# Gates moved into attention, cached values beside the branch products, and a third pass of the second out projection

## The chip, the cores and the metric

The kernel runs on one core of one Trainium2 chip. The metric is the device time in microseconds (us) of the whole program. The core has five engines with queues of their own, each of which works in order: PE multiplies matrices, DVE does element work on vectors, ACT does the same with functions and scales, POOL does it more slowly and also issues transfers, and SP only issues transfers. PE has two clock levels, 1.2 and 2.4 GHz; the profile gives the granted clock of a stretch as a share of the higher one.

## The reference, cut to what matters

One decoder layer, one inference step: a prompt of 1024 tokens and 8 samples of 4 new tokens each, whose earlier 1024 tokens lie in a paged cache.

```
proj   = x @ w_in                      # columns: q k v | HGRN q f i g | gate_a | gate_b
oA     = diff attention, 4 heads       # softmax(q1 k1) - lambda softmax(q2 k2), times v
         # samples: keys and values gathered from cache pages, 8 x 2 pages of each
oB     = HGRN2 recurrence, 4 heads
merged = sigmoid(gate_a) * (oA @ w_branch_a) + sigmoid(gate_b) * (oB @ w_branch_b)
h      = LayerNorm(ALPHA * x + merged @ w_out)
[a|g]  = h @ w_up;  c = causal conv3(a) + b
out    = LayerNorm(ALPHA * h + (gelu(c) * g) @ w_down)
```

Keys, values, the recurrent state and the last rows of the convolution (conv_p, conv_s) are outputs too.

## The kernel before

All data are float32. Each float32 product is made of three products of halves: a tile is split into a high part (`wh`, an ACT cast) and a low part (`wl`, a DVE subtraction), and high x high, low x high and high x low are added up (lines 238 to 240 for projections, 1147 to 1149 and 1248 to 1250 in the feed-forward part).

The kernel is written with a scheduler: the code issues instructions in program order, and the scheduler reorders them on each engine by their place in the program, their readiness as it models them, and the buffers of their pools. What has no buffer waits for one.

The stages follow each other. First come the turning of x, the HGRN heads and the projections, to about 405 us. Then the attention heads 0 to 3, to about 626 us, in which projections of the next head are the only other work for PE. A **gate** is one 128-column piece of gate_a or gate_b for all tokens: `do_gates(1)` issues 72 matmuls and their sigmoid. 16 of them exist. Before, one or two get among the attention heads by the scheduler's own doing and fourteen calls of `do_gates(1)` stand in a loop with the sample attention: in the first seven turns `sample.keys` (eight calls, one for each sample, two page gathers each), in the last seven `sample.values` (again eight). A gather (line 726) is an indirect transfer issued by POOL into the buffers `pg`, of which there are two; a page of values is used by 32 small matmuls (line 803).

The tokens are then worked on in two halves of 512 and 544 columns. `merge(Ot, half)` first makes the branch products (eight steps m, of which each multiplies both branches and adds them under the gates), and then the out projection `merged @ w_out` in two passes over the output columns (`hf` 0 and 1): each pass loads and splits its half of w_out (`w_B`) and goes over the token tiles. A tile's LayerNorm (line 1102, ACT) follows its second pass; the result h is turned, written to DRAM scratch (`hT`) and read again in quadrants for the feed-forward part, which uses seven products of sums of quadrants (B11, T2, B21, B22, T1, T3, T4) instead of eight plain ones. `up` runs over 22 column steps and two token chunks, `down_half` over 22 input steps for each half; its inputs come back from DRAM scratch (`r<-uT`, through two staging tiles). `ln2` is the final LayerNorm. For half 0 it is done by ACT (scale, line 1305) and POOL (gain and offset, lines 1306 and 1307), for half 1 mostly by DVE (lines 1311 and 1312). `conv_out` turns the convolution's last rows, copies them from PSUM to `co` on ACT (two buffers) and writes each `co` with two transfers; it is the last code of the program.

Of the kernel before, what the change touches and what calls it, by code (L numbers as in the profile page):

```python
# [44 lines left out]
def hybrid_step(ctx: ExitStack, tc: tile.TileContext, I, O):  # L45
# [797 lines left out]
    gates = [(3584, m, m) for m in range(8)] + [(4608, m, 8 + m) for m in range(8)]  # L843
# [94 lines left out]
    for i in range(14):  # L938
        do_gates(1)
        for b in range(8 * (i % 7) // 7, 8 * (i % 7 + 1) // 7):  # L940
            (sample.keys if i < 7 else sample.values)(b)
        if i == 6:
            aps.close()
        if i == 11:
            Ot = load_o(*HALVES[0][:2])
    avs.close()
    px.close()
    up[1] = ctx.enter_context(tc.tile_pool(name="upb", bufs=1))
    w2s, ups = ExitStack(), ExitStack()
    wx[0] = w2s.enter_context(tc.tile_pool(name="wx", bufs=1))  # L950

    rp = [ctx.enter_context(rpool("ra")), ups.enter_context(rpool("rb"))]
    h0 = ups.enter_context(rpool("h0"))
# [10 lines left out]
    def operands():  # L964
        c0 = []
        for o in range(7):
            pair = []
            for i in range(2):
                home = {(T4, 0): 0, (T4, 1): 1, (T3, 1): 4}.get((o, i))
                pair.append(h0.tile([128, 4, 256], F32R, name=f"h0_{o}{i}") if home is None else rt(home, (4, 256), F32R))  # L970
# [39 lines left out]
    def merge(Ot, half):  # L1010
# [5 lines left out]
        for m in range(8):  # L1016
            w = wunit([wview(wbb, m * 128, 128), wview(wba, m * 128, 128)])
            ga, gb_ = wide("ae"), wide("c")
            SY.dma_start(gb_[:, :nh], gsc[8 + m][:, th:th + nh])
            SY.dma_start(ga[:, :nh], gsc[m][:, th:th + nh])  # L1020
            for c0, cn in cks:
                cs = slice(c0, c0 + cn)
                pb, pa = pmm(), pmm()
                mm3(pb[:, :cn], [(w[k], (Ot[k][:, 0, cs], Ot[k][:, 1, cs])) for k in range(4)])
                mm3(pa[:, :cn], [(w[k], (Ot[k][:, 0, cs], Ot[k][:, 1, cs])) for k in range(4, 8)])
                V.scalar_tensor_tensor(gb_[:, cs], gb_[:, cs], 1.0, pb[:, :cn], ALU.add, ALU.mult)
                V.scalar_tensor_tensor(ga[:, cs], ga[:, cs], 1.0, pa[:, :cn], ALU.add, ALU.mult)
# [53 lines left out]
        for hf in range(2):  # L1081
            w = w_B(wout, hf * 512, 512)
            late = []
            for t, r in zip(tiles, rr):
                tt, tn = tok(t)
# [11 lines left out]
                if hf == 0:  # L1097
                    continue
# [9 lines left out]
    merge(Ot, 0)  # L1108
    Ot = load_o(*HALVES[1][:2])
    merge(Ot, 1)  # L1110

# [3 lines left out]
    def wcombos(m):  # L1115
# [12 lines left out]
        put(B11, a11)  # L1128
        G.tensor_tensor(s1, a21, a22, ALU.add)
        G.tensor_tensor(s2, s1, a11, ALU.subtract)  # L1130
        put(T2, s2)
        put(B21, a12)
        put(T1, s1)
        G.tensor_tensor(a11, a11, a21, ALU.subtract)
        put(T3, a11)
        G.tensor_tensor(a12, a12, s2, ALU.subtract)
        put(B22, a12)
# [15 lines left out]
    for m in range(NM):  # L1153
# [8 lines left out]
        for c, cn in enumerate(CHUNK):  # L1162
# [18 lines left out]
            V.tensor_tensor(u3, m1, product(w, x, T3, cn), ALU.add)  # L1181
            G.tensor_tensor(gg[:, 1, o:o + cn], u3, m5, ALU.add)
            conv_in(1, u4, product(w, x, B22, cn))
            V.tensor_tensor(gg[:, 0, o:o + cn], u3, product(w, x, T4, cn), ALU.add)
            if m + c == 0:

                while pending:
                    pending.pop(0)()
                for t in (2, 3):
                    tile_operands(t)  # L1190
# [19 lines left out]
    us = ctx.enter_context(rpool("us"))  # L1210
# [5 lines left out]
    def ut(k):  # L1216
# [3 lines left out]
        return qt((0, 1, 2, 3, 4, 5, 8, 9, 10, 11, 6, 7, 12, 13, 14, 15)[k - 6])  # L1220

    def down_half(half):
# [3 lines left out]
        for k in range(NM):  # L1226
            if k % 2 == 0:
                raw = rt(2 + k // 2 % 2, (2, 544))
# [57 lines left out]
        def ln2(i0, i1):  # L1286
# [10 lines left out]
            for i in range(i0, i1):  # L1297
# [4 lines left out]
                np_ = D if i == 4 or not half else 512 if i == 1 else 0  # L1302
# [6 lines left out]
                for c in range(0, D - np_, 512):  # L1309
# [3 lines left out]
                    SY.dma_start(y[:, c], r[:, c])  # L1313

        down((0, 1), cks)
        for m in range(2, KD - 2 if half else KD):
            down((m,), cks)
        if half:
# [6 lines left out]
        else:  # L1325
            ln2(0, 4)

    down_half(0)
    down_half(1)


# [90 lines left out]
```

## Time and profile before

| | |
|---|---|
| device time, median of 3 runs | 1865.85 us (1859.72 to 1867.9) |
| the profiled execution, its own time | 1858.9 us |
| its span in the trace | 1857.1 us |
| PE busy | 1732.4 us, 93% of the span |
| DVE, ACT, POOL busy | 60%, 41%, 32% |
| mean granted PE clock | 0.967 |
| DMA | 213 MB, mean 115 GB/s |

The share of PE is an average over stages with different limits. A busy PE can also be a slow one, so the clock is read beside it; matmuls are pipelined, so their pace is read from how many start in a stretch and not from the duration of one. Idle time of the other engines costs nothing while PE works.

### The profile page before, as it was taken

The page shows a single profiled execution, that of the slowest core. Times are in us where ns is not written, and L with a number is a line of the kernel's source. Part 1 is how long each engine was busy: PE and PEld are TensorE (multiplying, and loading weights), DVE is VectorE, ACT ScalarE, POOL GpSimd, SP SyncE. Part 2 cuts the span into 40 slices and gives each one's busy share as a digit, 9 for nine tenths or more (in the row PEclk, how much of TensorE's full clock was granted, in tenths as well). Part 3 has the DMA queues.
Part 4 walks back from the last instruction along what each step waited for, and adds up shares of the span by engine and source line. Part 5 has one row for each costly group of instructions (what it writes and reads, how often), then busy time and mean ns, then how long its engine had stood idle before and what let it go on. Part 6 is the DMA issues. An engine that isn't in the chain of part 4 may idle for free.

```text
span 1857.1 us, 34326 instructions
## 1 busy us (share of the span) xinstructions
PE 1732.4 (93%) x13412; PEld 1620.2 (87%) x13412; DVE 1117.9 (60%) x2297; ACT 770.1 (41%) x1771; POOL 594.1 (32%) x736
## 2 busy tenths in 40 slices
PE   8999999998998989898979859999999997998995
PEld 8999999997987989786879659999999996887995
DVE  5767555656668555115556777777766776336435
ACT  6466253445646512212243444444434444225222
POOL 0000110432322222112121467766676662003203
PEclk9999999998999999998989969999999998999998
DMA  6120211220210277676566232222322227435543
GB/s 210 35 59 25 81 59 45 85 70 27 78 36 13 98 272 252 235 232 216 162 207 184 64 99 84 84 76 70 92 76 76 70 88 234 127 108 169 157 125 108
DMA packets 214122, 212.99 MB, mean 115 GB/s; under 512 B 11084, under 2 KB 182046, under 8 KB 209864
## 3 DMA queue, kind: packets, MB, share of 16 engines
q1 hardware_dynamic: 189856, 133.95, 23.7%
q0 software_dynamic: 16976, 67.99, 10.5%
q10 hardware_dynamic: 7128, 8.86, 1.4%
q8 instruction: 106, 1.74, 0.4%
q14 instruction: 56, 0.46, 0.1%
HBM read 170.34 MB, written 40.41 MB: 113 GB/s over the span
## 4 chain that ended last, share of the span: by engine, by line
PE 78%; DMA 8%; DVE 4%; issue 4%; ACT 2%; POOL 2%; SPq 0%; ACTq 0%; POOLq 0%; DVEq 0%
PE mm L238 10%; PE mm L239 10%; PE mm L240 10%; PE mm L1147 4%; PE mm L1149 4%; PE mm L1148 4%; PE mm L1250 3%; PE mm L1249 3%; PE mm L1248 3%; PE tp L220 3%; DMA pg<-in_cache_k_dram,idx 2%; PE tp L1147 2%; PE tp L1148 2%; PE tp L1149 2%; PE ps_s L1147 2%
## 5 line engine op out<-in xcount | busy, mean ns | idle before, releaser
L133 DVE TENSOR_TENSOR wl<-raw,wh 128x512 fp32r<-128x512 f32 x370 | 272.4, 743 | 244.1 <-ACT wh L132 229.7
L132 ACT CAST wh<-raw 128x512 fp32r<-128x512 f32 x370 | 222.1, 608 | 295.2 <-PE mm L1249 119.2
L238 PE MATMUL mm<-xh,wh 128*128 128x384 f32 (+1 forms) x560 | 187.2, 335 | 0.3 <-ACT wh L132 0.3
L239 PE MATMUL mm<-xl,wh 128*128 128x384 f32 (+1 forms) x560 | 186.2, 333 | 0.0
L240 PE MATMUL mm<-xh,wl 128*128 128x384 f32 (+1 forms) x560 | 186.1, 333 | 0.0
L238 PE MATMUL mm<-wh,xh 128*128 128x256 f32 x480 | 137.0, 286 | 1.4 <-DVE rb L581 1.3
L239 PE MATMUL mm<-wl,xh 128*128 128x256 f32 x480 | 137.0, 286 | 0.2 <-DVE wl L133 0.2
L240 PE MATMUL mm<-wh,xl 128*128 128x256 f32 x480 | 136.2, 285 | 0.0
L1250 PE MATMUL mm<-q,wl 128*128 128x512 f32 (+2 forms) x384 | 125.7, 329 | 5.2 <-DVE wl L133 5.2
L1248 PE MATMUL mm<-q,wh 128*128 128x512 f32 (+2 forms) x384 | 125.2, 326 | 0.3 <-ACT wh L132 0.3
L1249 PE MATMUL mm<-q,wh 128*128 128x512 f32 (+2 forms) x384 | 125.0, 326 | 0.0
L240 PEld LDWEIGHTS mm<-xh,wl 128*128 128x128 f32 x560 | 105.7, 189 | 3.6 <-issue 3.5
L238 PEld LDWEIGHTS mm<-xh,wh 128*128 128x128 f32 x560 | 105.6, 189 | 2.9 <-issue 2.0
L239 PEld LDWEIGHTS mm<-xl,wh 128*128 128x128 f32 x560 | 105.9, 189 | 2.0 <-issue 1.8
L238 PEld LDWEIGHTS mm<-wh,xh 128*128 128x128 f32 x480 | 91.1, 190 | 2.9 <-issue 1.5
L239 PEld LDWEIGHTS mm<-wl,xh 128*128 128x128 f32 x480 | 91.1, 190 | 1.2 <-DVE wl L133 0.6
L240 PEld LDWEIGHTS mm<-wh,xl 128*128 128x128 f32 x480 | 91.2, 190 | 0.1
L1257 POOL DMA_DIRECT2D c<-hT x24 | 12.9, 539 | 220.4 <-PE tp L220 91.7
L1250 PEld LDWEIGHTS mm<-q,wl 128*128 128x128 f32 x384 | 73.1, 191 | 10.9 <-DVE wl L133 5.6
L1147 PE MATMUL mm<-h,wh 128*128 128x256 f32 x264 | 75.0, 284 | 5.2 <-ACT h L132 5.2
L1248 PEld LDWEIGHTS mm<-q,wh 128*128 128x128 f32 x384 | 73.2, 191 | 5.8 <-ACT wh L132 0.5
L1249 PEld LDWEIGHTS mm<-q,wh 128*128 128x128 f32 x384 | 73.2, 191 | 5.7 <-DVE q L133 0.4
(496 smaller groups left out, 5517.0 us busy)
## 6 DMA issues: line engine op xcount, KB each, us to landing
raw<-in_w_in_dram SPq DMA_DIRECT2D x44, 512.0 KB, 3.8
raw<-in_w_up_dram SPq DMA_DIRECT2D x44, 512.0 KB, 4.9
raw<-in_w_down_dram SPq DMA_DIRECT2D x36, 512.0 KB, 3.9
raw<-in_w_out_dram SPq DMA_DIRECT2D x16, 512.0 KB, 3.5
raw<-in_w_down_dram SPq DMA_DIRECT2D x18, 384.0 KB, 3.5
gsc<-gt ACTq DMA_DIRECT2D x32, 192.0 KB, 2.5
r<-uT SPq DMA_DIRECT2D x22, 272.0 KB, 3.8
uT<-ae POOLq DMA_DIRECT2D x22, 256.0 KB, 2.4
```

Source lines behind the costliest of these rows:

```text
L132: S.copy(h, src)
L133: eng.tensor_tensor(l, src, h.bitcast(F32), ALU.subtract)
L220: PE.transpose(out, in_, ident[:n, :n])
L238: PE.matmul(ps, lhsT=ah, rhs=bh, start=(i == 0), stop=False)
L239: PE.matmul(ps, lhsT=ah, rhs=bl, start=False, stop=False)
L240: PE.matmul(ps, lhsT=al, rhs=bh, start=False, stop=(i == n - 1))
L1147: PE.matmul(ps, lhsT=ah, rhs=bh, start=(k == 0), stop=False)
L1148: PE.matmul(ps, lhsT=ah, rhs=bl, start=False, stop=False)
L1149: PE.matmul(ps, lhsT=al, rhs=bh, start=False, stop=(k == 3))
L1248: PE.matmul(ps, lhsT=ah, rhs=bh, start=(k == 0), stop=False)
L1249: PE.matmul(ps, lhsT=ah, rhs=bl, start=False, stop=False)
L1250: PE.matmul(ps, lhsT=al, rhs=bh, start=False, stop=(k == NM - 1))
```

## The change

Six edits. Three gates are issued after head 0 and two after head 1 of the attention, and the loop of the sample attention has nine gates left: they go with the eight calls for keys and the first two for values. The gates' order changes from all gate_a first to gate_a and gate_b in turn. The other six calls for values are made inside `merge` of half 0, after every second branch step (four) and after two tiles of the out projection's first pass. The out projection of half 1 goes in three passes: columns 0 for tiles 4 and 5, columns 1 for all tiles, columns 0 for tiles 8, 6 and 7; w_out's first half is loaded and split twice for it. The seven products are made in another order. The final LayerNorm of half 0's prompt tiles goes from ACT and POOL to DVE, piece by piece in the turns of half 1's loop, with its stores on POOL's queue. The feed-forward part's staging gets a third tile, and to make room `co` has one buffer instead of two.

```diff
-    gates = [(3584, m, m) for m in range(8)] + [(4608, m, 8 + m) for m in range(8)]
+    gates = [(3584 + 1024 * i, m, 8 * i + m) for m in range(8) for i in range(2)]
...
     attn(0, Q[0], K[0], v[0])
+    do_gates(3)
     K1 = proj_k(1, k_slots())
     vsl = tok_slots()
     attn(1, Q[1], K[1], v[1])
     v = proj_tok(1024, 1, vsl, vs_, O["v_p"], O["v_s"])
+    do_gates(2)
...
-    for i in range(14):
+    steps = [(sample.keys, b) for b in range(8)] + [(sample.values, b) for b in range(8)]
+    def beside(n):
+        for f, b in steps[:n]:
+            f(b)
+        del steps[:n]
+        if len(steps) == 8:
+            aps.close()
+    for n in (2, 1, 1, 1, 1, 1, 1, 1, 1):
         do_gates(1)
-        for b in range(8 * (i % 7) // 7, 8 * (i % 7 + 1) // 7):
-            (sample.keys if i < 7 else sample.values)(b)
...
+        beside(n)
...
-    def merge(Ot, half):
+    def merge(Ot, half, beside=None):
...
+            if beside and m % 2:
+                beside(1)
-        tiles = (8, 4, 5, 6, 7) if half else tiles
+        tiles = (4, 5, 8, 6, 7) if half else tiles
...
-        for hf in range(2):
+        for hf, some in ((0, tiles[:2]), (1, tiles), (0, tiles[2:])) if half else ((0, tiles), (1, tiles)):
             w = w_B(wout, hf * 512, 512)
             for t, r in zip(tiles, rr):
+                if t not in some:
+                    continue
...
-                if hf == 0:
+                if t not in done:
+                    done.add(t)
+                    if beside and t % 2:
+                        beside(1)
                     continue
...
     merge(Ot, 1)
+    tile_operands(2)
...
             S.copy(m1, product(w, x, B11, cn))
-            p6 = product(w, x, T2, cn)
             conv_in(0, m1, product(w, x, B21, cn))
-            V.tensor_tensor(m1, m1, p6, ALU.add)
+            p3 = product(w, x, B22, cn)
             S.copy(m5, product(w, x, T1, cn))
+            V.tensor_tensor(m1, m1, product(w, x, T2, cn), ALU.add)
...
             if k % 2 == 0:
-                raw = rt(2 + k // 2 % 2, (2, 544))
+                j = k // 2 % 3
+                raw = rt(j + 1, (2, 544)) if j else us.tile([128, 2, 544], F32, tag="ur", name="ur")
...
-                co = us.tile([18, 512], F32, tag="co", name="co", bufs=2)[:, :mn * 128]
+                co = us.tile([18, 512], F32, tag="co", name="co")[:, :mn * 128]
...
-                np_ = D if i == 4 or not half else 512 if i == 1 else 0
+                np_ = D if i == 4 else 512 if half and i == 1 else 0
...
-                    SY.dma_start(y[:, c], r[:, c])
+                    (SY if half else G).dma_start(y[:, c], r[:, c])
...
         for m in range(2, KD - 2 if half else KD):
             down((m,), cks)
+            if half:
+                before(m - 2, m - 1)
...
-        else:
-            ln2(0, 4)
-
-    down_half(0)
-    down_half(1)
+        return ln2
+
+    down_half(1, down_half(0))
```

**PE in the last third of attention head 0.** `scp` are the scores, `tp<-s` the turned probabilities (line 220) and their products with the values (line 665), and `mm` projections. Before, from the largest score block on:

```order
2389 L665 MATMUL tp<-s_4123,s_4609 128x128 x4
2390 L637 MATMUL scp<-s_3300,s_3733 128x512
2391 L638 MATMUL scp<-s_3302,qpad_141 128x512
...
2398 L665 MATMUL tp<-s_4123,s_4609 128x128 x2
2399 L220 MATMUL tp<-ident,s_4648 128x128 x7
2400 L637 MATMUL scp<-s_3303,s_3735 128x128
```

And now, at the same block:

```order
2407 L665 MATMUL tp<-s_4123,s_4564 128x128
2408 L220 MATMUL tp<-ident,s_4601 128x128 x4
2409 L239 MATMUL mm<-xl,wh 128x384
2410 L240 MATMUL mm<-xh,wl 128x384
2411 L637 MATMUL scp<-s_3300,s_3733 128x512
...
2415 L238 MATMUL mm<-xh,wh 128x384
2416 L239 MATMUL mm<-xl,wh 128x384
2417 L637 MATMUL scp<-s_3301,s_3734 128x512
```

Between the attention's own matmuls stand gate matmuls (`mm<-xh,wh`) where nothing stood; 216 of them lie in rows 2262 to 2528.

**PE behind the last sample key.** `tp<-pg,aT` are the products with pages of values (32 to a page) and `mm<-q` branch products of half 0. Before, the first two of the values are followed by a gate:

```order
3903 L796 MATMUL tp<-vs__120,an 32x512 x4
3904 L803 MATMUL tp<-pg,aT 32x128 x32
3905 L238 MATMUL mm<-xh,wh 128x384
3906 L239 MATMUL mm<-xl,wh 128x384
```

Now the last gate ends among them, and the branch begins behind two and a half pages:

```order
4240 L796 MATMUL tp<-vs__120,an 32x512 x4
4241 L803 MATMUL tp<-pg,aT 32x128 x32
4242 L239 MATMUL mm<-xl,wh 128x288
...
4252 L240 MATMUL mm<-xh,wl 128x288
4253 L803 MATMUL tp<-pg,aT 32x128 x48
4254 L238 MATMUL mm<-q_8697,wh 128x512
```

The pages moved from between gates of 72 matmuls to a place with 11 matmuls between them, and the later ones into the branch products.

**ACT at the end of the program.** Rows of before, the copies to `co` and the transfers of them:

```order
1496 L216 COPY rt_19534<-tp 128x2x128 x2
1497 L216 COPY co<-tp 18x512 x2
1498 L1283 DMA out_dram<-co 2x512
1499 L1284 DMA out_dram<-co 16x512
1500 L1283 DMA out_dram<-co 2x512
1501 L1284 DMA out_dram<-co 16x512
1502 L216 COPY co<-tp 18x512
```

And now:

```order
1456 L216 COPY rt_19548<-tp 128x2x128 x2
1457 L216 COPY co<-tp 18x512
1458 L1302 DMA out_dram<-co 2x512
1459 L1303 DMA out_dram<-co 16x512
1460 L216 COPY co<-tp 18x512
```

Two copies stood ahead of the first transfer, and now one stands ahead of each pair; the rest of the engine's order at the end is the same.

## Rows read from the trace of the kernel before

**Rows 1.** Stretches: length, busy of each engine (count), PE clock, DMA share, GB/s.

```profile
430.00:460.00 30.00, 22.57 (x135) 19.35 (x134) 19.22 (x76) 15.62 (x50) 7.87 (x17) 0.83 0.07 27
460.00:520.00 60.00, 60.00 (x488) 58.88 (x487) 37.25 (x107) 38.06 (x125) 20.49 (x42) 1.00 0.20 64
520.00:540.00 20.00, 15.86 (x104) 14.05 (x104) 9.51 (x30) 5.24 (x19) 5.61 (x11) 0.83 0.07 27
...
640.00:660.00 20.00, 20.00 (x128) 20.00 (x127) 9.21 (x13) 7.65 (x15) 8.54 (x11) 1.00 0.81 300
...
860.00:890.00 30.00, 30.00 (x132) 24.29 (x130) 21.45 (x30) 9.59 (x17) 9.58 (x7) 1.00 0.67 213
...
1055.00:1110.00 55.00, 25.14 (x156) 23.45 (x155) 43.04 (x62) 23.85 (x50) 38.57 (x35) 0.70 0.31 87
1110.00:1545.00 435.00, 435.00 (x3552) 435.00 (x3552) 321.23 (x576) 193.08 (x427) 288.38 (x312) 1.00 0.26 80
...
1685.00:1720.00 35.00, 28.40 (x202) 27.35 (x201) 25.21 (x32) 16.61 (x27) 19.21 (x9) 0.90 0.47 150
```

**Rows 2.** What PE waited for, whole span: releaser, us in total, times, longest.

```profile
PE tp L1147 <- ACT q L132: 11.7, 1, 11.7
PE tp L803 <- DMA pg<-in_cache_v_dram,idx: 10.1, 3, 7.0
PE mm L1248 <- ACT x L132: 8.4, 1, 8.4
...
PE tp L220 <- DVE s L683: 7.1, 2, 3.6
...
PE mm L1147 <- ACT h L132: 5.2, 1, 5.2
```

**Rows 3.** The same, between 1020 and 1120 us.

```profile
PE tp L220 <- ACT r L1102: 8.0, 1, 8.0
```

**Rows 4.** PE's groups between 757 and 893 us, shapes apart: busy, mean ns.

```profile
L239 PE MATMUL mm<-q,wh 128*128 128x512 f32 x64 | 25.9, 404 | 0.0
L240 PE MATMUL mm<-xh,wl 128*128 128x384 f32 x72 | 24.6, 342 | 0.0
...
L240 PE MATMUL mm<-xh,wl 128*128 128x288 f32 x40 | 11.9, 299 | 0.0
```

**Rows 5.** PE's timeline at one sample's values: start us, duration us, instruction.

```profile
803.19 1.06 PE L796 MATMUL tp<-vs__120,an 32*32 32x512 f32 x8
804.18 1.95 PE L803 MATMUL tp<-pg,aT 128*32 128x128 f32 x64
```

**Rows 6.** Pages of values, 740 to 870 us: landing, then the gather queue's transfers.

```profile
DMA to landing us min/median/max: 5.5/7.5/10.6
...
q0 software_dynamic: 2514, 17.90, 39.5%
```

**Rows 7.** The stretch between 650 and 660 us, columns as in rows 1.

```profile
650.00:660.00 10.00, 10.00 (x65) 10.00 (x64) 5.73 (x8) 3.26 (x7) 2.02 (x5) 1.00 0.92 359
```

**Rows 8.** DMA issues of the page: KB each, median us to landing.

```profile
uT<-ae POOLq DMA_DIRECT2D x22, 256.0 KB, 2.4
```

**Rows 9.** DVE between 1700 and 1720 us, and between 1720 and 1825 us.

```profile
L133 DVE TENSOR_TENSOR wl<-raw,wh 128x512 fp32r<-128x512 f32 x4 | 9.1, 2302 | 0.0
...
L133 DVE TENSOR_TENSOR wl<-raw,wh 128x512 fp32r<-128x512 f32 x38 | 28.4, 746 | 49.9 <-ACT wh L132 48.0 <-PE mm L1249 1.6
```

**Rows 10.** POOL's line 1306 over the span, and DVE's line 1311.

```profile
L1306 POOL TENSOR_TENSOR rt<-rt,lnrow x6: 1270/2460/2856, 1702.8 to 1844.7; 128x1024 f32<-128x1024 f32 x4, 32x1024 f32<-32x1024 f32 x1, 128x512 f32<-128x512 f32 x1
...
L1311 DVE SCALAR_TENSOR_TENSOR rt<-rt,mv,lnrow 128x512 f32<-128x512 f32 x7 | 4.9, 728 | 0.0
```

**Rows 11.** ACT and its queue from 1838 us: start us, us, idle before.

```profile
1840.28 0.57 ACT L216 COPY co<-tp 18x512 f32<-18x512 f32 x1 [0.48 <-PE tp L220]
...
1843.38 0.57 ACT L216 COPY co<-tp 18x512 f32<-18x512 f32 x1 [1.67 <-DMA out_dram<-co]
...
1844.27 0.36 ACTq L1284 DMA_DIRECT2D out_dram<-co  x1
...
1846.52 0.57 ACT L216 COPY co<-tp 18x512 f32<-18x512 f32 x1 [1.20 <-DMA out_dram<-co]
...
1847.85 0.36 ACT L216 COPY co<-tp 18x256 f32<-18x256 f32 x1 [0.76 <-DMA out_dram<-co]
...
1848.53 0.32 ACTq L1284 DMA_DIRECT2D out_dram<-co  x1
```

More of the change, by code (lines that the diff above doesn't have):

```diff
@@ L937, in hybrid_step @@
     sample = SampleAttn(ap, av)
-    for i in range(14):
-        do_gates(1)
-        for b in range(8 * (i % 7) // 7, 8 * (i % 7 + 1) // 7):
-            (sample.keys if i < 7 else sample.values)(b)
-        if i == 6:
-            aps.close()
-        if i == 11:
+    steps = [(sample.keys, b) for b in range(8)] + [(sample.values, b) for b in range(8)]
[6 more added lines that the diff above has]
+    for n in (2, 1, 1, 1, 1, 1, 1, 1, 1):
+        do_gates(1)
+        if len(gates) == 2:
             Ot = load_o(*HALVES[0][:2])
-    avs.close()
+        beside(n)
     px.close()
[L948 to L953, printed above, removed]
+    w2s, ups, h0 = ExitStack(), ExitStack(), []
+    rp = [ctx.enter_context(rpool("ra"))]
+    up[1] = ctx.enter_context(rpool("upb"))
+    wx[0] = w2s.enter_context(rpool("wx"))
+    rp.append(ups.enter_context(rpool("rb")))
     B11, T2, B21, B22, T1, T3, T4 = range(7)
@@ L969, in operands @@
                 home = {(T4, 0): 0, (T4, 1): 1, (T3, 1): 4}.get((o, i))
-                pair.append(h0.tile([128, 4, 256], F32R, name=f"h0_{o}{i}") if home is None else rt(home, (4, 256), F32R))
+                pair.append(h0[0].tile([128, 4, 256], F32R, name=f"h0_{o}{i}") if home is None else rt(home, (4, 256), F32R))
             c0.append(pair)
@@ L1080, in merge @@
         sts = f2.tile([128, 5, 2, 6], F32, tag="bst", name="bst")
-        for hf in range(2):
+        done, late = set(), []
+        for hf, some in ((0, tiles[:2]), (1, tiles), (0, tiles[2:])) if half else ((0, tiles), (1, tiles)):
             w = w_B(wout, hf * 512, 512)
-            late = []
             for t, r in zip(tiles, rr):
+                if t not in some:
+                    continue
                 tt, tn = tok(t)
@@ L1106, in merge @@
         pending.extend((lambda x=x: turn_(*x)) for x in late)
-    merge(Ot, 0)
+    merge(Ot, 0, beside)
+    avs.close()
+    h0.append(ups.enter_context(tc.tile_pool(name="h0", bufs=1)))
     Ot = load_o(*HALVES[1][:2])
     merge(Ot, 1)
+    tile_operands(2)
     w_up, w_dn = I["w_up"][0], I["w_down"][0]
@@ L1128, in wcombos @@
         put(B11, a11)
+        put(B21, a12)
         G.tensor_tensor(s1, a21, a22, ALU.add)
         G.tensor_tensor(s2, s1, a11, ALU.subtract)
+        G.tensor_tensor(a12, a12, s2, ALU.subtract)
+        put(B22, a12)
+        put(T1, s1)
         put(T2, s2)
-        put(B21, a12)
-        put(T1, s1)
         G.tensor_tensor(a11, a11, a21, ALU.subtract)
         put(T3, a11)
-        G.tensor_tensor(a12, a12, s2, ALU.subtract)
-        put(B22, a12)
         put(T4, a22)
@@ L1175, in hybrid_step @@
             S.copy(m1, product(w, x, B11, cn))
-            p6 = product(w, x, T2, cn)
             conv_in(0, m1, product(w, x, B21, cn))
-            V.tensor_tensor(m1, m1, p6, ALU.add)
+            p3 = product(w, x, B22, cn)
             S.copy(m5, product(w, x, T1, cn))
+            V.tensor_tensor(m1, m1, product(w, x, T2, cn), ALU.add)
             G.tensor_tensor(u4, m5, m1, ALU.add)
             V.tensor_tensor(u3, m1, product(w, x, T3, cn), ALU.add)
+            conv_in(1, u4, p3)
             G.tensor_tensor(gg[:, 1, o:o + cn], u3, m5, ALU.add)
-            conv_in(1, u4, product(w, x, B22, cn))
             V.tensor_tensor(gg[:, 0, o:o + cn], u3, product(w, x, T4, cn), ALU.add)
@@ L1188, in hybrid_step @@
                     pending.pop(0)()
-                for t in (2, 3):
-                    tile_operands(t)
+                tile_operands(3)
         for hf, tag in enumerate(("ae", "c")):
@@ L1209, in hybrid_step @@
     wx[0] = None
-    us = ctx.enter_context(rpool("us"))
+    us = ctx.enter_context(tc.tile_pool(name="us", bufs=1))
     zp = ctx.enter_context(tc.tile_pool(name="z", bufs=1))
@@ L1219, in ut, with down_half @@
             return us.tile([128, 2, 544], F32R, tag=f"x{k}", name=f"x{k}")
-        return qt((0, 1, 2, 3, 4, 5, 8, 9, 10, 11, 6, 7, 12, 13, 14, 15)[k - 6])
-    def down_half(half):
+        return qt((0, 1, 4, 5, 6, 7, 8, 9, 2, 3, 10, 11, 12, 13, 14, 15)[k - 6])
+    def down_half(half, before=None):
         th, nh, tiles, cks = HALVES[half]
```

## The prediction, made before the changed kernel ran

> **What bounds the kernel now.** I read the stretches first [rows 1]. From 1110 to 1545 us PE is busy all 435 us at full clock: nothing that happens on another engine there can change the time. The room lies in the stretches where PE is idle or its clock is down. As a measure of what a stretch loses I take its length less busy time times granted clock; it is rough, since the clock of idle parts counts in it. Attention head 0's end, 430 to 460 us: 30 − 22.57 × 0.83 = 11.3 us. Head 1's end, 520 to 540 us: 20 − 15.86 × 0.83 = 6.8 us. Between them, 460 to 520 us, where projections stand beside the head, PE is busy all 60 us at clock 1.00. The step from the second out projection to `up`, 1055 to 1110 us: 55 − 25.14 × 0.70 = 37.4 us. The start of the second `down`, 1685 to 1720 us: 35 − 28.40 × 0.90 = 9.4 us.
>
> Then I read what PE waited for [rows 2, 3]: 11.7 us and 5.2 us for operands of `up`'s first products, 8.0 us between 1020 and 1120 us for the LayerNorm of a tile, 8.4 us for inputs at the start of `down`, 10.1 us in three waits for pages of values, and 7.1 us in two waits for DVE at the ends of attention heads. Last comes the end of the program, where ACT copies and stores `co` [rows 11].
>
> **Part 1: five gates among the attention heads.** A gate is 72 matmuls; 128 gate matmuls start in 20 us [rows 1], so one takes 72 × 20/128 = 11.3 us. The gates' work stays what it is; five of them move to where PE has 18.1 us to give (11.3 + 6.8). By the order, head 0's end now has gate matmuls between its own, as 460 to 520 us had projections, where nothing was lost. I keep back 3 us, under half of the 7.1 us that PE waits at the heads' ends for the norm on DVE, because the order puts nothing new on DVE's side of that chain: **−15 us**, bounds −18 (all filled) and 0 (the heads only get longer). Before, the gates covered the sample attention; the keys keep seven gates for eight calls, so their stretch is priced at 0.
>
> **Part 2: values beside the branch.** The stretch from 757 to 893 us holds 3 × 72 + 3 × 40 = 336 gate matmuls and 3 × 64 branch matmuls [rows 4] (a line each for the three products; one missing record counted in). At the pace of gates (20/128 = 0.156 us) and of the branch (30/132 = 0.227 us [rows 1]) these take 52.4 and 43.6 us. Of 136 us 40 are left for the values. Their own matmuls take 1.95 us for the two pages of a sample, and 1.06 us for eight opening ones [rows 5], which stand at two of eight samples: about 18 us. So 22 us are waits (10.1 of them named [rows 2]), slow clock and turns between shapes. Now six samples of eight have branch or out-projection work beside them. Four branch pairs give 48 × 0.227 = 10.9 us between two samples, and a page lands in 5.5 to 10.6 us, 7.5 at the median [rows 6]: hidden, with little to spare. But behind the last key, two and a half pages and then more stand with 11 gate matmuls (1.7 us) between them and two buffers `pg`: the third and fourth page can only be asked for when the first two are used. That is one exposed landing and part of a second, 7.5 + 4, and some 4 us of slow clock as in the present waits. Beyond that the branch carries more traffic: 213 GB/s now [rows 1] make 2.3 MB in 10.9 us, two pages add 2.2 MB (17.90 MB for 16 [rows 6]), 4.5 MB in 10.9 + 2 us, or 350 GB/s, where the fastest stretch moved 359 [rows 7]. I allow 2 us for each of four pairs. 11.5 + 4 + 8 = 23.5 against 22: I take **+2 us**; bounds −12 (only the one landing exposed, 7.5 + 2.5 left of the 22) and +20 (see the rivals).
>
> **Part 3: three passes.** A pass over one tile is 24 matmuls, 5.4 us; the third pass now holds tiles 8, 6 and 7, so tiles 4 and 5 have both passes, their LayerNorm and their turn behind them some 16 us earlier. The tile that ends last is still tile 7, with the LayerNorm wait behind it (8.0 us [rows 3]); what is gained is that the operands which need tiles 4 and 5 no longer queue with those of tiles 6 and 7 on DVE (43.04 of 55 us busy) and POOL (38.57). The new order of products asks for T1 to T4, which need sums of quadrants, after B11, B21 and B22. So the 11.7 us wait should go, and the 8.0 and 5.2 stay: **−12 us**; bounds 0 and −25 (11.7 + 8.0 + 5.2). The extra w_out half costs eight splits on ACT and DVE, 0.75 us each on DVE [rows 9], beside matmuls; if that cover were gone, 6 us. In the steady part the order of products changes nothing, since PE has no idle time there.
>
> **Part 4: `down`.** A third staging tile lets one pair of `down`'s inputs load earlier; the other two tiles come free no earlier than now, and the pairs behind still wait for them: of the 8.4 us wait [rows 2] I take **−2**, bounds 0 and −8. At half 1's start POOL's line 1306 runs 2.46 us at the median [rows 10], and DVE's splits beside it take 2302 ns where they take 746 later [rows 9]; five such splits lose some 8 us of DVE time. Half 0's LayerNorm on DVE costs 16 operations of 0.73 us [rows 10], 11.7 us, in nearly the same place, but without the slow ones beside them. Of the 9.4 us I take **−5**; bounds −9 and +3 (the 11.7 us less the 8 on the splits' way).
>
> **Part 5: one `co`.** Now a copy waits for the landing of the `co` two before. The copy at 1843.38 is followed by its second store at 1844.27, and the copy which needs that buffer starts at 1846.52 [rows 11]: 3.1 us from copy to copy of one buffer. With one buffer all six copies stand in this chain: the last would start at 1840.28 + 5 × 3.14 = 1856.0 instead of 1847.85. Nothing lies behind it that could take this up, as its store at 1848.53 is the last of the program: **+8 us**, bounds +6 and +9.
>
> **Sum.** −15 + 2 − 12 − 2 − 5 + 8 = −24 us. Against the profiled execution, 1858.9 − 24 = 1835 us; that execution lies 7 us under the median of the runs, from which it would be 1842. I take 1839.
>
> **A rule that speaks against the change.** Gathers, and now stores of half 0's LayerNorm, are issued by POOL while DVE is busy. In the rows DVE is busy 321 of 435 us from 1110 to 1545 us [rows 1], and the stores of `uT` that POOL issues there land in 2.4 us for 256 KB [rows 8]; so I give contention with DVE no price. The Trainium skill ("SBUF — State Buffer", section "A bandwidth-pool intuition that's wrong") says that a transfer issued by GpSimd waits for its descriptors while VectorE holds the port they share, about 3100 ns instead of 620 in its example. By the skill's figures, an estimate, two gathers a sample would land 5 us later and the sum would be about −24 + 6 × 5 = +6; the way it would take is that of rival (a).
>
> **Rivals.**
> (a) The gathers don't hide beside the branch; this one ends on the other side. Gathers are issued by POOL in its order, behind the additions of a branch step, and share the DMA with branch weights and gate rows near the fastest rate seen. If each of the six samples exposed the whole median landing of 7.5 us and half of it came again as slow clock and late splits, the price is 6 × 11 = 66 us less the 8 counted for the pairs in part 2: 1839 + 58 = 1897 us. It decides where it costs 27 us more than the 8 counted (1866, the median), 6 us a sample. For it speaks the 350 of 359 GB/s; against it, that in the present stretch only three of 16 pages are waited for.
> (b) The end of the out projection is bound by tile 7, and all operands of chunk 1 by it: part 3 gives nothing, 1851 us. For it: the 8.0 us wait; against it: 11.7 us fall on one wait for an ACT cast, late in the queue.
> (c) The change doesn't do what it seems to do in attention: the scheduler's place for the gates delays scores, and the heads' chain through ACT and DVE gets longer by what PE gains. Part 1 gives 3 us: 1851 us. Against it: the 60 busy us from 460 to 520.
> (d) More hides than I count: parts 1 to 3 at −18, −12 and −20: 1839 − 25 = 1814 us.
>
> **Chances.** Forecast 0.50; (a) 0.13, of which half goes over the bound; (b) 0.14; (c) 0.11; (d) 0.12. The measurement tells half a per cent (9 us) from no change. Faster by more than that means under 1856.5: the forecast nearly whole (0.47), (b) and (c) in three cases of five (0.15), (d) whole: 0.74. Slower, over 1875: 0.09 from (a) and its neighbours. Same: 0.17. The forecast's own range is 1826 to 1852, from the bounds of its terms; for eight in ten I go down to (d) and up to where (a) is half true: 1814 to 1864.
>
> **What would show it.** Part 1: PE busy without gaps at the ends of heads 0 and 1, clock 1.00. Part 2: a wait of PE for pages of about 7 to 12 us behind the last key, and none over 3 us beside branch products. Part 3: the wait of `up` for an ACT cast under 3 us, that for the last tile's LayerNorm still near 8. Part 4: no split of w_down over 1.2 us at the start of half 1. Part 5: six copies to `co` 3.1 us apart at the very end, and the span ending some 9 us behind the last. Wrong it would be through waits for pages beside branch products, or through a longer way from tile 7 to `up`.

## The result and the profile after

The changed kernel takes 1842.53 us at the median of four runs (1839.93 to 1843.06), the kernel before 1864.11 in the same comparison: ratio 0.9882, interval 0.9857 to 0.9908. Timed once more (the run `c1_changed_again` below) it is 0.9902, 0.9883 to 0.9920. So it is faster by about 1%, some 20 us; the forecast was 1839. Its profiled execution took 1842.59 us with a span of 1840.1 us, 17.0 us under the span of before.

The total came out near the forecast, the terms did not. First the waits of PE in the changed kernel, over the whole span (releaser, us in total, times, longest):

```profile
PE ps_s L1166 <- ACT q L132: 14.6, 1, 14.6
PE mm L1267 <- ACT x L132: 12.8, 1, 12.8
PE tp L803 <- DMA pg<-in_cache_v_dram,idx: 9.1, 4, 3.5
PE tp L220 <- ACT r L1118: 9.1, 2, 6.9
...
PE tp L220 <- DVE s L683: 2.1, 1, 2.1
```

The two waits for DVE at the ends of heads 0 and 1, the 7.1 us of [rows 2], are gone: from 400 to 597 us PE waits 0.2 us in all, and the 2.1 us of the last row stand at 641.6 us, at the end of head 2. The 8.0 us wait for the last tile's LayerNorm [rows 3] is gone too: between 1000 and 1110 us no wait of PE is for a LayerNorm. But the first row answers to the 11.7 us of [rows 2], the wait for the operands of a product of `up`, and it has grown to 14.6; so has that at the start of `down`, from 8.4 to 12.8 us. The waits for pages are 9.1 instead of 10.1.

Stretches of the changed kernel, with the columns of [rows 1]:

```profile
440.00:470.00 30.00, 30.00 (x228) 29.84 (x226) 12.37 (x39) 11.30 (x30) 4.88 (x9) 1.00 0.21 69
...
535.00:560.00 25.00, 25.00 (x180) 24.79 (x179) 7.91 (x27) 10.47 (x26) 1.67 (x1) 1.00 0.17 53
...
598.00:664.00 66.00, 50.60 (x306) 42.51 (x306) 46.74 (x160) 37.09 (x109) 9.49 (x24) 0.90 0.03 9
...
795.00:820.00 25.00, 17.46 (x222) 13.83 (x221) 2.97 (x7) 5.07 (x9) 4.76 (x5) 0.73 0.68 240
820.00:870.00 50.00, 48.31 (x349) 37.62 (x348) 24.89 (x44) 13.54 (x26) 17.08 (x14) 1.00 0.88 307
...
1040.00:1110.00 70.00, 43.11 (x233) 39.52 (x232) 47.91 (x81) 30.52 (x62) 40.17 (x39) 0.73 0.25 72
...
1660.00:1710.00 50.00, 49.60 (x335) 46.08 (x334) 39.56 (x78) 24.27 (x44) 9.90 (x14) 1.00 0.67 217
```

PE is busy all the time at clock 1.00 where heads 0 and 1 now end (440 to 470 and 535 to 560 us). Around the first pages of values (795 to 820) it loses 25 − 17.46 × 0.73 = 12.3 us by the measure of the prediction. Beside the branch it loses under 2 us in 50, with the DMA at 307 GB/s. The step to `up` (1040 to 1110) still loses 70 − 43.11 × 0.73 = 38.5 us. The start of half 1's `down` (1660 to 1710) has no loss left.

The whole attention can be measured without the rough clock. These stretches run from its first score product to its last, with the products of line 238 alone (their count is the first in brackets). Before:

```profile
370.10:620.20 250.10, 88.42 (x305) 58.09 (x304) 0.95 0.13 42
```

After:

```profile
369.70:663.50 293.80, 124.43 (x417) 78.37 (x416) 0.98 0.17 54
```

112 products of line 238 came in, so with lines 239 and 240 it is 336 gate matmuls, 52.5 us at the 0.156 us of the prediction. The attention became 43.7 us longer: 8.8 us of the gates went into its gaps. In the profile of c1 it takes 291.9 us, so 10.7 went in.

To cut the program in two places that both kernels have, here are the first products of a kind and their first and last start: those of `up` (L1147 before, L1166 after) and of `down` (L1248, L1267). Before:

```profile
L1147 PE MATMUL mm<-h,wh x264: 277/281/582, 1056.8 to 1533.1; 128*128 128x256 f32 x132
...
L1248 PE MATMUL mm<-q,wh x384: 275/295/481, 1562.1 to 1832.4; 128*128 128x256 f32 x101, 128*128 128x512 f32 x64, 128*128 128x288 f32 x27
```

After:

```profile
L1166 PE MATMUL mm<-h,wh x264: 276/279/582, 1044.6 to 1523.7; 128*128 128x256 f32 x132
...
L1267 PE MATMUL mm<-q,wh x384: 275/295/628, 1556.2 to 1815.0; 128*128 128x256 f32 x112, 128*128 128x512 f32 x64, 128*128 128x288 f32 x16
```

All that lies ahead of `up` became 12.2 us shorter (1056.8 to 1044.6). `up` became 2.8 us longer (476.3 to 479.1). From there to the last such product of `down` it is 8.0 us less (299.3 to 291.3). What follows to the end of the span takes 24.7 and 25.1 us. The sum is −12.2 + 2.8 − 8.0 + 0.4 = −17.0. These are single executions. The kernels of e1, e2, e3, e8, e10 and c1 below are the changed kernel up to the end of `up`; in their profiles the first product of `up` starts at 1041.4 to 1050.2 us, and `up` takes 475.0 to 478.3. So the first of the four numbers is known to some 5 us only, and the 2.8 us cannot be told from nothing. Two terms of the prediction are missing in it: the 12 us of the three passes, and the 8 us that the single `co` was to cost.

Here is the end of the program, ACT and its queue in the changed kernel:

```profile
1822.93 0.57 ACT L216 COPY co<-tp 18x512 f32<-18x512 f32 x1 [0.48 <-PE tp L220]
...
1825.79 0.57 ACT L216 COPY co<-tp 18x512 f32<-18x512 f32 x1 [2.29 <-DMA out_dram<-co]
...
1828.41 0.57 ACT L216 COPY co<-tp 18x512 f32<-18x512 f32 x1 [1.33 <-DMA out_dram<-co]
...
1836.67 0.36 ACT L216 COPY co<-tp 18x256 f32<-18x256 f32 x1 [1.99 <-DMA out_dram<-co]
...
1837.34 0.32 ACTq L1303 DMA_DIRECT2D out_dram<-co  x1
```

The copies do stand in one chain, some 2.75 us apart, and take 13.7 us from the first to the last instead of 7.6 [rows 11]. But the span ends 2.8 us behind the start of the last store, where before it ran on for 8.6 us. What both ends have in common is their distance from POOL's last instruction. Before:

```profile
1846.09 1.59 POOL L1307 TENSOR_TENSOR rt<-rt,lnrow 128x512 f32<-128x512 f32 x1
```

After:

```profile
1828.73 1.59 POOL L1326 TENSOR_TENSOR rt<-rt,lnrow 128x512 f32<-128x512 f32 x1
```

It ends at 1847.68 and 1830.32, the spans at 1857.1 and 1840.1: 9.4 and 9.8 us later. The trace names what POOL has in that time: a DRAIN, at one of the last lines of the program (min, median and max duration in ns, then the first and last start). Before:

```profile
L1418 POOLq DRAIN  x3: 46/97/10293, 1846.1 to 1856.9; - x3
```

After:

```profile
L1437 POOLq DRAIN  x3: 46/97/10625, 1828.7 to 1839.8; - x3
```

The longest of the three is the first. It ends at 1856.3 and 1839.3, that is 8.7 and 9.0 us behind POOL's last instruction and 0.8 us ahead of the end of the span.

### The profile page after: what moved, and what is told of

Its sections match the earlier page's. It is cut to its first block, busy times and chain, and to the rows that moved or that the text cites. A ratio compares the mean times of both kernels' runs of the same rounds, so it can differ in the third digit from the quotient of the medians.

```text
span 1840.1 us, 34341 instructions
## 1 busy us (share of the span) xinstructions
PE 1730.7 (94%) x13412; PEld 1618.0 (88%) x13412; DVE 1103.8 (60%) x2327; ACT 765.5 (42%) x1775; POOL 579.4 (31%) x735
## 4 chain that ended last, share of the span: by engine, by line
PE 48%; DMA 7%; DVE 4%; issue 3%; ACT 2%; POOL 1%; SPq 0%; ACTq 0%; POOLq 0%; DVEq 0%
PE mm L1268 4%; PE mm L1267 4%; PE mm L1269 4%; PE mm L1168 4%; PE mm L1167 4%; PE mm L1166 4%; PE mm L238 3%; PE mm L239 3%; PE mm L240 3%; PE ps_s L1167 2%; PE ps_s L1168 2%; PE ps_s L1166 2%; PE tp L1167 2%; PE tp L1168 2%; PE tp L1166 2%
## 5 line engine op out<-in xcount | busy, mean ns | idle before, releaser
L132 ACT CAST wh<-raw 128x512 fp32r<-128x512 f32 x378 | 226.7, 609 | 405.5 <-PE mm L1268 116.7
L1267 PE MATMUL mm<-q,wh 128*128 128x512 f32 (+2 forms) x384 | 124.8, 325 | 0.0
L1269 PE MATMUL mm<-q,wl 128*128 128x288 f32 (+2 forms) x384 | 124.7, 326 | 0.1
L1167 PE MATMUL mm<-h,wh 128*128 128x256 f32 x264 | 75.8, 287 | 3.4 <-DVE h L133 3.4
L1166 PE MATMUL mm<-h,wh 128*128 128x256 f32 x264 | 75.6, 286 | 2.5 <-ACT wh L132 2.5
L1267 PEld LDWEIGHTS mm<-q,wh 128*128 128x128 f32 x384 | 72.5, 189 | 5.7
```

Of the source, the lines that this page charges most:

```text
L132: S.copy(h, src)
L1166: PE.matmul(ps, lhsT=ah, rhs=bh, start=(k == 0), stop=False)
L1167: PE.matmul(ps, lhsT=ah, rhs=bl, start=False, stop=False)
L1267: PE.matmul(ps, lhsT=ah, rhs=bh, start=(k == 0), stop=False)
L1269: PE.matmul(ps, lhsT=al, rhs=bh, start=False, stop=(k == NM - 1))
```

## The experiments

All were timed in up to five rounds with the kernel before on the same chip; the ratios below are to it. The changed kernel's own ratios are 0.9882 and 0.9902. A difference of 0.003 (5 to 6 us) between two ratios is within what their intervals leave open. e1 to e8 ran on one chip, e9 to e11 and c1 on another.

**e1_two_co: two buffers for the copies again.**

```diff
-                co = us.tile([18, 512], F32, tag="co", name="co")[:, :mn * 128]
+                co = (us.tile([18, 512], F32, tag="co", name="co") if m0 % 8 else
+                      us.tile([128, 2, 544], F32, tag="ur", name="ur").rearrange("p a t -> p (a t)")[:18])[:, :mn * 128]
```

> The changed kernel, and every second copy of conv_out goes to the staging tile `ur`, which is free by then: two buffers in turn again. Theory as predicted (the chain of copies through one buffer sets the end): the last copy comes 6 us earlier, as before the change, and the time falls by 6 to 8 us. Rival (something else ends the program, since the span of before ran on for 8.6 us behind its last store and that of the changed kernel for 2.8 us): the last copy comes 6 us earlier and the time falls by under 1 us, with some 8 us of nothing behind the last store.

Measured: 1844.49 us, ratio 0.9900 (0.9877 to 0.9922): no gain. The copies took 7.6 us from first to last, as before the change, and the last store came early, but the span ended at 1844.9, 8.9 us behind its start and 9.8 us behind POOL's last instruction (1833.56 + 1.59):

```profile
1833.56 1.59 POOL L1326 TENSOR_TENSOR rt<-rt,lnrow 128x512 f32<-128x512 f32 x1
...
1835.97 0.32 ACTq L1303 DMA_DIRECT2D out_dram<-co  x1
```

**e2_no_pool_ln2: the last LayerNorm piece on DVE.**

```diff
-                np_ = D if i == 4 else 512 if half and i == 1 else 0
+                np_ = D if i == 4 else 0
```

> The changed kernel with one `co`, but the last piece of the final LayerNorm goes to DVE instead of ACT and POOL, so that POOL's last work comes some 5 us earlier. Theory that POOL's last work sets the end: the chain of copies takes over at once, so the time falls by under 1 us. Theory as predicted (the copies set the end): the time stays, within 1 us. It tells the two apart only together with the next run.

Measured: 1843.48 us, 0.9893 (0.9871 to 0.9916), no gain either. POOL's last work now starts at 1828.75 and the copies set the end: the span ends at 1843.7, 2.6 us behind the start of the last store.

```profile
1828.75 1.13 POOL L367 TENSOR_TENSOR rs<-mv,mhalf 128x2 f32<-128x2 f32 x1 [5.53 <-DVE mv L1313]
...
1841.08 0.32 ACTq L1303 DMA_DIRECT2D out_dram<-co  x1
```

**e3_two_co_no_pool: both.** The diffs of e1 and e2 together.

> Both edits of the two runs ahead. Theory that POOL's last work holds the end of the program back by some 9 us: both holds are gone and the time falls by 3 to 6 us. Theory as predicted: the same 6 to 8 us as with two buffers alone, so nothing more from the move to DVE. Third possibility: a fixed stretch at the end that neither edit touches, no change in either.

Measured: 1836.04 us, 0.9859 (0.9835 to 0.9882). Neither edit alone gave anything, both together give 7 to 8 us against each of them on the same chip. The traces put 4.3 us of this at the end: from the last product of `down` to the end of the span it takes 20.8 us, where the changed kernel and e1 take 25.1 and e2 24.8. The rest lies ahead of `up`, where the three kernels are the same, and is within the spread named above. The span ends at 1833.7, again 9.8 us behind POOL's last instruction (1822.78 + 1.13), and 4.0 us behind the start of the last store:

```profile
1822.78 1.13 POOL L367 TENSOR_TENSOR rs<-mv,mhalf 128x2 f32<-128x2 f32 x1 [5.53 <-DVE mv L1313]
...
1829.74 0.32 ACTq L1303 DMA_DIRECT2D out_dram<-co  x1
```

```profile
L1267 PE MATMUL mm<-q,wh x384: 275/295/628, 1552.2 to 1812.9; 128*128 128x256 f32 x112, 128*128 128x512 f32 x64, 128*128 128x288 f32 x16
```

**e10_late_pool: one tiny POOL instruction more, at the very end.** The kernel of e3, and:

```diff
                 S.dma_start(O["conv_s"][:, c], co[2:18])
+            G.tensor_copy(f2.tile([18, 1], F32, name="zz"), co[:, :1])
```

> Two buffers for the copies and the last LayerNorm piece on DVE, as in the third run, and then one copy of a single column on POOL that reads the last `co` (added work that computes nothing needed). Theory that the program ends some 9.8 us behind POOL's last instruction: this one starts about 8.4 us behind the last POOL work of the third run's tail at the same place, so the end moves by 5 to 7 us, back to the changed kernel's time or over it. Rival, the end follows the last store: within 1 us of the third run.

Measured: 1845.84 us, 0.9921 (0.9902 to 0.9939), against 0.9859 for e3. One copy of 0.18 us, whose result nobody reads, costs 0.6% by these ratios. By the traces it costs 5.7 us (0.3%) at the end, 26.5 us behind the last product of `down` instead of 20.8; the rest lies where the two kernels are the same. It starts late, and POOL's DRAIN comes behind it:

```profile
1833.70 0.18 POOL L1304 COPY zz<-co 18x1 f32<-18x1 f32 x1 [5.53 <-ACT co L216]
...
1833.95 0.32 ACTq L1303 DMA_DIRECT2D out_dram<-co  x1
```

```profile
L1267 PE MATMUL mm<-q,wh x384: 277/295/628, 1555.1 to 1817.2; 128*128 128x256 f32 x112, 128*128 128x512 f32 x64, 128*128 128x288 f32 x16
...
L1438 POOLq DRAIN  x3: 46/97/9198, 1833.7 to 1843.4; - x3
```

The copy ends at 1833.88; the span ends at 1843.7, 9.8 us later. The four kernels settle the question: the program ends 9.8 us behind POOL's last instruction, by way of POOL's DRAIN, or some 2.5 us behind the start of the last store, whichever is later.

**e4_gates_back: the five gates out of the attention.**

```diff
-    do_gates(3)
...
-    do_gates(2)
...
+    do_gates(5)
     for n in (2, 1, 1, 1, 1, 1, 1, 1, 1):
```

> The changed kernel, but the five gates are not among the attention heads; they are issued in one piece ahead of the sample attention. Theory of part 1: heads 0 and 1 lose their cover again, slower by 10 to 15 us (1853 to 1858 us). Rival (c), the heads only get longer by what PE gains: slower by at most 3 us.

Measured: 1846.14 us, 0.9917 (0.9898 to 0.9936): 3 to 7 us over the changed kernel, by ratios whose intervals overlap. So it decides for neither. Its stretches (columns as above) and two of its waits:

```profile
430.00:460.00 30.00, 22.45 (x135) 19.17 (x134) 19.10 (x76) 15.69 (x51) 7.86 (x17) 0.83 0.07 27
520.00:540.00 20.00, 15.92 (x100) 14.28 (x99) 9.13 (x29) 4.95 (x19) 5.62 (x11) 0.74 0.07 27
...
640.00:740.00 100.00, 99.55 (x1169) 93.42 (x1168) 44.32 (x54) 25.47 (x51) 25.03 (x47) 1.00 0.69 237
```

```profile
PE tp L220 <- DVE s L683: 7.0, 2, 3.6
...
PE ps_s L752 <- DVE pw L746: 0.4, 1, 0.4
```

The losses at the ends of heads 0 and 1 are back (11.4 and 8.2 us; 11.3 and 6.8 before). What makes up for part of it is that the five gates now cover the sample's keys: the wait for the transposed keys falls to 0.4 us, from 7.0 in the kernel before and 5.3 in the changed one, and PE runs from 640 to 740 us almost without loss. So the gates are worth what they cover, in either place. That the attention is the better one is not shown: the first product of `up` starts at 1048.2 us here, inside the 1041.4 to 1050.2 of the kernels that have them there.

**e5_two_passes: two passes again.**

```diff
-        tiles = (4, 5, 8, 6, 7) if half else tiles
+        tiles = (8, 4, 5, 6, 7) if half else tiles
...
-        for hf, some in ((0, tiles[:2]), (1, tiles), (0, tiles[2:])) if half else ((0, tiles), (1, tiles)):
+        for hf, some in ((0, tiles), (1, tiles)):
```

> The changed kernel with the second out projection in two passes over all tiles in the order 8, 4, 5, 6, 7, as before; the order of products stays. Theory as predicted (the early tiles' turn in three passes is worth 12 us): slower by 8 to 15 us. Rival (b), tile 7's way through LayerNorm, turn, scratch and sums sets the start of chunk 1 whatever comes earlier: within 3 us of the changed kernel, and the wait of about 15 us for chunk 1's first operand is still there.

Measured: 1841.73 us, 0.9894 (0.9878 to 0.9909): the time of the changed kernel. The third pass is worth nothing that can be measured. It does take away the wait for the last tile's LayerNorm, which is back here with 5.8 us, but PE then waits longer for chunk 1's first operand, 14.6 us in place of 12.6. `up` takes 477.4 us from first to last start, as in the changed kernel's profiles:

```profile
PE ps_s L1166 <- ACT q L132: 12.6, 1, 12.6
PE tp L220 <- ACT r L1118: 5.8, 1, 5.8
```

```profile
L1166 PE MATMUL mm<-h,wh x264: 276/279/415, 1046.0 to 1523.4; 128*128 128x256 f32 x132
```

**e6_direct_tiles: tiles 6 and 7 combined on the chip.** In the changed kernel the turned tiles 4 and 5 go into the sums of quadrants directly, while 6 and 7 are stored to DRAM and read back.

```diff
-            elif t in (4, 5):
+            elif t >= 4:
                 tile_operands(t - 4, *yy)
...
     merge(Ot, 1)
-    tile_operands(2)
...
                     pending.pop(0)()
-                tile_operands(3)
```

> The changed kernel, but the turned tiles 6 and 7 are combined straight from the on-chip tiles, as tiles 4 and 5 are, instead of being read back from the scratch in DRAM; the stores to it stay, since `down` reads them. Theory (b): the stores and the read-back stand on tile 7's way, 3.0 us and 4.5 us with their queues, so the 14.6 us wait shrinks to about 6 and the time falls by 5 to 9 us. Rival: DVE and POOL set that way with their splits and sums, and the time stays within 2 us. Second rival: the held tiles `hs` delay the first products of `up`, slower by 2 to 6 us.

Measured: 1834.96 us, 0.9852 (0.9834 to 0.9871), 6 to 9 us faster than the changed kernel. The wait is 4.5 us instead of 14.6, and `up` takes 467.4 us, 7.6 us less than the shortest `up` of the changed kernel's code. The edit takes the read-back away and also lets the sums stand earlier in the program; the run does not part the two:

```profile
PE ps_s L1165 <- ACT q L132: 4.5, 1, 4.5
```

```profile
L1165 PE MATMUL mm<-h,wh x264: 276/279/418, 1047.1 to 1514.5; 128*128 128x256 f32 x132
```

**e11_order_back: the products in the order of before.**

```diff
             S.copy(m1, product(w, x, B11, cn))
+            p6 = product(w, x, T2, cn)
             conv_in(0, m1, product(w, x, B21, cn))
-            p3 = product(w, x, B22, cn)
+            V.tensor_tensor(m1, m1, p6, ALU.add)
             S.copy(m5, product(w, x, T1, cn))
-            V.tensor_tensor(m1, m1, product(w, x, T2, cn), ALU.add)
...
-            conv_in(1, u4, p3)
...
+            conv_in(1, u4, product(w, x, B22, cn))
```

(the weights' sums go back to their order too)

> The changed kernel with the seven products and the combination of weights in the order of before (B11, T2, B21, T1, T3, B22, T4). Theory as predicted (PE has no idle time in the steady part; the order matters at the start of `up` only, as part of the 12 us): slower by 0 to 4 us. Rival: with the early tiles ready sooner, the sums T are wanted before they can be there, slower by 5 to 10 us.

Measured: 1833.57 us, 0.9856 (0.9835 to 0.9876), where the changed kernel on the same chip has 0.9902 (0.9883 to 0.9920): faster, which neither theory expected. Its trace shows two shorter waits: that for chunk 1's operand is 9.0 us, and that at the start of `down` 8.8, where the changed kernel's profiles have 12.2 and 12.8. The products of `up` take 474.2 us from first to last, against 476.6 and 479.1 in those two profiles.

```profile
PE tp L1166 <- ACT q L132: 9.0, 1, 9.0
PE mm L1267 <- ACT x L132: 8.8, 1, 8.8
```

```profile
L1166 PE MATMUL mm<-h,wh x264: 276/279/562, 1044.1 to 1518.3; 128*128 128x256 f32 x132
```

That is 2.4 to 4.9 us of the 8 between the medians, and hardly beyond the spread of 475.0 to 479.1. The profiles are of the slowest execution here (1836.20) and of the fastest of c1 (1836.72), so most of the gain cannot be placed in them and stays open.

**e7_values_with_gates: no values beside branch and out projection.**

```diff
-    for n in (2, 1, 1, 1, 1, 1, 1, 1, 1):
+    for n in (2, 2, 2, 2, 2, 2, 2, 1, 1):
...
-    merge(Ot, 0, beside)
+    merge(Ot, 0)
```

> The changed kernel, but no values beside branch and out projection: the nine gates take all sixteen calls, two each for seven gates and one each for two. Theory of part 2 (branch work covers what the five gates covered before): without it the gathers of 32 pages stand beside 9 gates, and waits for pages grow; slower by 8 to 20 us. Rival: what the values cost in waits is only moved, and nine gates do as well as gates and branch together: within 3 us.

Measured: 1846.08 us, 0.9921 (0.9907 to 0.9934): 4 to 7 us over the changed kernel, less than the 8 to 20 of the first theory. The interval reaches that of c1, and the first product of `up` starts at 1047.7 us, inside the spread named above, so the rival's 3 us is not excluded. PE's waits in it, 640 to 960 us:

```profile
PE tp L803 <- DMA pg<-in_cache_v_dram,idx: 8.5, 4, 3.6
...
PE ps_s L752 <- DVE pw L746: 8.0, 4, 5.7
```

The waits for values are the same as with the branch's cover (8.5 against 9.1 us), those for keys larger by 2.7 us. Nine gates nearly suffice for the sixteen calls of the eight samples.

**e8_ln2_act_pool: half 0's LayerNorm back on ACT and POOL.**

```diff
-                np_ = D if i == 4 else 512 if half and i == 1 else 0
+                np_ = D if i == 4 or not half else 512 if i == 1 else 0
...
-            if half:
-                before(m - 2, m - 1)
...
-        return ln2
-    down_half(1, down_half(0))
+        if not half:
+            ln2(0, 4)
+    down_half(0)
+    down_half(1)
```

> The changed kernel, but the final LayerNorm of half 0 goes back to ACT and POOL in one piece at the end of half 0, with its stores on SP. Theory of part 4: splits of w_down beside POOL's work take over 2 us again and half 1 starts 5 to 9 us later; slower by 5 to 8 us. Rival: the third staging tile is what took the stall away; within 2 us.

Measured: 1847.10 us, 0.9923 (0.9906 to 0.9941), 4 to 8 us over the changed kernel. From the last product of `up` to that of `down` it takes 297.4 us (1522.7 to 1820.1) against 291.3. DVE's splits of w_down from 1660 to 1720 us in it:

```profile
L133 DVE TENSOR_TENSOR wl<-raw,wh 128x512 fp32r<-128x512 f32 x17 | 23.0, 1371 | 7.4 <-ACT wh L132 7.4
```

And in the changed kernel from 1660 to 1710 us:

```profile
L133 DVE TENSOR_TENSOR wl<-raw,wh 128x512 fp32r<-128x512 f32 x15 | 10.3, 685 | 7.1 <-ACT wh L132 7.1
...
L1331 DVE SCALAR_TENSOR_TENSOR rt<-rt,rs,lnrow 128x512 f32<-128x512 f32 x8 | 5.7, 748 | 0.0
L1330 DVE SCALAR_TENSOR_TENSOR rt<-rt,mv,lnrow 128x512 f32<-128x512 f32 x8 | 5.7, 746 | 0.0
```

In the changed kernel DVE does 11.4 us more work of its own, and no split takes over 0.7 us. The mean of 1371 ns in e8 hides two kinds. Here are seven splits in a row:

```profile
1697.04 17.99 DVE L133 TENSOR_TENSOR wl<-raw,wh 128x512 fp32r<-128x512 f32 x7 [5.28 <-ACT wh L132]
...
1715.65 0.68 DVE L133 TENSOR_TENSOR wl<-raw,wh 128x512 fp32r<-128x512 f32 x1
```

The seven stand beside POOL's gain and offset (lines 1325 and 1326, from 1693.2 to 1714.5 us) and take 2.6 us each. The next one, behind POOL's last, takes 0.68.

**c1_changed_again and e9_direct_and_end: the changed kernel once more, and with what the runs pointed to.** e9 has the diffs of e1, e2 and e6.

> The changed kernel once more, on the same chip as the next three, so that they can be held against it. Ratio to before near 0.988.

> The changed kernel with the tiles 6 and 7 combined on the chip, two buffers for the copies of conv_out, and the last piece of the final LayerNorm on DVE. Both theories (read-back on tile 7's way; POOL's last work holds the end) speak of different places, so the gains add up: 10 to 15 us under the changed kernel, about 1830 us, ratio near 0.983. If one of them was noise: 4 to 7 us under it.

Measured: the changed kernel 1841.80 us, 0.9902 (0.9883 to 0.9920); e9 1829.12 us, 0.9826 (0.9805 to 0.9847). The two gains add up, 12.7 us between the medians, 30 us under the kernel before. In e9's trace `up` takes 467.6 us, as in e6, and the end behind the last product of `down` 20.8, as in e3. The old order of products on top of it was not tried.

## Why the prediction came out, and where it failed

**Part 1, −15.** Right in its mechanism, and 4 to 6 us too large. The losses at the ends of heads 0 and 1 are gone, as the prediction wanted it, with clock 1.00. But the attention took only 9 to 11 us of the gates into its gaps. What is missing to 15 lies in heads 2 and 3, where I expected no difference: the stretch from 598 to 664 us loses 66 − 50.60 × 0.90 = 20.5 us, where before 565 to 620 us lost 13.6 by the same measure (45.47 us busy at clock 0.91). Why was not tried. The other 3 us that came off ahead of `up` are within its spread. Run e4 adds a limit to the term: as far as it can tell, the gates would have earned most of it among the sample's keys as well.

**Part 2, +2.** Right within what the trace can show. The page waits are 9.1 us where 7 to 12 behind the last key were forecast: 7.5 us in three pieces of at most 3.5 us ahead of the first branch product, and one of 1.6 us beside branch products. Rival (a) did not happen: pages of values landed in 8.0 us at the median (5.6 to 9.9) with the DMA at 307 GB/s, under the 10.9 us between two samples. Nor did the wait that the Trainium skill tells of ("SBUF — State Buffer", section "A bandwidth-pool intuition that's wrong") show: transfers issued by GpSimd (POOL), with VectorE (DVE) busy half of the time beside them, landed 0.5 us later than before, not 2.5. The trace does not tell whether VectorE held the shared port. Run e7 shows that the branch's cover was worth at most 7 us, not the tens that rival (a) put at stake.

**Part 3, −12.** Wrong, and rival (b) was what happened. The failing step is "the 11.7 us wait should go, and the 8.0 and 5.2 stay". It came out the other way round: the 8.0 us wait went, and the 11.7 grew to 14.6. I had the 11.7 us down to the early tiles' operands queuing with those of tiles 6 and 7. It was the late tiles' own way: LayerNorm, turn, store, read-back, sums. All waits of PE between 1000 and 1110 us add up to 29.8 us before and 27.5 after, so what went ahead of them came back behind. Runs e5 and e6 show it from both sides: taking the third pass away changes nothing in the time, and combining tiles 6 and 7 on the chip takes 10.1 us off the wait. The order of products, which I priced as part of these 12 us, cost some 8 us by the medians instead (e11).

**Part 4, −2 and −5.** Right in the sum, −8.0 measured against −7, and wrong in the split. At the start of half 0 the wait grew by 4.4 us (8.4 to 12.8). With the old order of products it is 8.8 (e11), so the growth goes with that order; what the third staging tile did alone was not tried. At half 1's start the whole loss of 9.4 us went; e8 puts 4 to 8 us of it down to the LayerNorm's move, with splits at 0.7 us in place of the 2.6 that they take beside POOL's.

**Part 5, +8.** Wrong. The chain through one `co` is there and 6.2 us longer; the failing step is "nothing lies behind it that could take this up". Before, the span ran on for 8.6 us behind the last store's start, and I read that tail as a fixed piece that moves along. It was POOL's DRAIN (e1, e2, e3 and e10), and the longer copies filled it.

That the forecast of 1839 held is luck in part, since two errors have opposite signs: the three passes brought 12 to 15 us less than I counted, and the single buffer cost 7.6 us less. With the passes and the buffer put right the sum would have been −24 + 14.8 − 7.6 = −16.8 us against the −17.0 of the spans; this closeness is chance too, since single sections spread by more. The range of 1826 to 1852 is also narrower than the bounds that it is said to come from: these add up to −66 and +32 us.

## What to carry to other kernels

Look at what lies between the last store and the end of the span before pricing an edit at the end: here it was longer than a store takes, because an engine that seemed done ended the program, and the edit on the other engine cost almost nothing. Where many operands are late, shorten the way of the last one (here its trip through DRAM) before moving the early ones further ahead. Work that covers a wait is worth only the difference between the waits that it can cover: the same five gates earned nearly as much among the keys as in the attention.

## What the runs showed of the hardware that I had not expected

The program ended 9.7 to 9.8 us behind the end of POOL's last instruction in ten of the fourteen profiles (among them the changed kernel's two, e1, e3, e9 and e10) and 9.4 us in that of before. In the ten it did not matter whether that instruction took 1.59 us (the changed kernel) or 0.18 us (e10). The time is that of POOL's DRAIN, which ends 8.7 us behind that instruction before and 9.0 us in the changed kernel and e10; what it waits for the views do not show. In e2, e7 and e8 the end came 2.3 to 2.6 us behind the start of the last store. A single-column copy on POOL that started late thus cost 5.7 us at the end of this kernel, and with two buffers for the copies POOL's earlier last work gained 4.3 us there.

A 128x512 subtraction on DVE took 0.68 us alone and 2.6 us on the mean of seven beside POOL's work with `lnrow` (e8).
